# Both heads' probabilities normalised on ScalarE in the attention overlays

## The chip, the core and the metric

The kernel runs on one core of a Trainium2 chip. A core has TensorE (PE, matmuls; PEld is its weight load), VectorE (DVE), ScalarE (ACT), GpSimd (POOL) and SyncE (SP, which here only issues DMAs). Each works through its own queue in order, and they wait for each other by semaphores. The metric is the device time of one execution in microseconds, as the median over runs.

## What is computed

One layer of a decoder trunk over 2048 tokens of width 1024: a modulation by a condition vector, one wide projection, sliding-window attention with sinks beside a pooling branch, three more projections and a layer norm. The attention is the part that matters here:

```
u = x * (1 + scale) + shift
q, k, v, a_gate, p_in, p_gate, m_a, m_p = split(u @ w_in)
logits = q . k / 8 + bias            # 16 heads of 64, 2 kv heads, window 128, blocks of 128
probs  = softmax(concat(logits, sink))[..., :-1]
a      = (probs . v) * silu(a_gate)
y      = (sigmoid(m_a) * (a @ w_attn_proj) + sigmoid(m_p) * (p @ w_pool_proj)) @ w_out * (1 + gate)
out    = layer_norm(2 ** 0.25 * x + y)
```

## The kernel before

The large products are computed in fp32 by three matmuls on a high and a low part of each operand, and blocked by a Winograd scheme of seven products per two-by-two block. The activations lie in seven sets in SBUF (`set_B11` and so on), each split in a high and a low part; the weights come by DMA into `W`, POOL makes the sums and differences that the scheme needs (`W<-W`, `W<-W,A`), ACT makes the high part (`act.copy`, a cast into `w_set`) and DVE, at a few places POOL, the low part (`low`, a subtraction `w_set<-W,w_set`). As soon as the low part of the first pair is made, POOL's next difference of `W` (`mid`) may begin, since it overwrites what the split has read. The products accumulate in PSUM (`mm`, `c`, `lg`, `p` by names), and ACT and DVE take them out: `q_hi`, `q_lo`, `sig`, `px`.

A planner (`plan`) decides on which product each weight load and split is issued. `run` walks through the products; some hooks and deferred steps are issued after each.

The attention doesn't have a stage of its own. `overlay` lays it into the projection's products: `beat` is called after every three matmuls of a product, and now and then issues one `step(n)`. There are two overlays, one for each half of the tokens, with 64 steps each; a step is one pair of heads and one block of 128 queries. In the trace the first runs from about 170 to 490 us, the second from about 758 to 1075 us. `step(n)` works on four blocks at once, in this order of issue:

- PE: scores of block n into the PSUM tile `lg` (one buffer; it waits until DVE has read the scores of block n-1), the transposes of block n-2 into `pt`, and the product of block n-3 with `v` into `pv`.
- Block n-1, the lines that are changed: DVE makes the reciprocals of both heads' sums (`sm`, 128x2); ACT multiplies head 0's probabilities by the first, DVE head 1's by the second. `E` is the tile named `L` in the profile, 128 queries by 2 heads by 257 values.
- Block n-2: ACT copies the transposed probabilities to `pth` (high part).
- Block n-3: ACT copies the lower half of `pv` to `o2` (`o` in the profile).
- Block n, for both heads in turn: DVE adds the bias to the scores and takes the minimum (`tensor_tensor_reduce`; the page prints it as CUSTOM_DVE, the order as ISA), which frees `lg`; ACT takes the exponential with the sum in an accumulator.
- DVE: low part `ptl` of block n-2, and the sums `st` of block n-3.
- POOL copies the sink's value into `L` of block n+1.

Nearly every engine instruction is recorded by the helper at line 56, so all rows carry L56 and are told apart by their tiles.

## Time and profile before

| | us |
|---|---|
| median of 3 runs (1715.05 to 1715.85) | 1715.49 |
| profiled execution | 1721.38 |
| its span, first to last instruction | 1719.3 |
| clock granted to TensorE, mean | 0.989 |

A row of the groups reads: line, engine, operation, output<-inputs by the program's names, shapes, count, then busy us and mean ns of one, then the idle time of the engine ahead of them and who ended it. A row in order of time begins with the start in us and the duration; in brackets stands the idle time before it and who ended that. A row of the waits reads: who waited, for whom, us in total, times, longest. The clock is the share of full speed that TensorE was granted.

### The profile page before, as it was taken

The page shows a single profiled execution, that of the slowest core. Times are in us where ns is not written, and L with a number is a line of the kernel's source. Part 1 is how long each engine was busy: PE and PEld are TensorE (multiplying, and loading weights), DVE is VectorE, ACT ScalarE, POOL GpSimd, SP SyncE. Part 2 cuts the span into 40 slices and gives each one's busy share as a digit, 9 for nine tenths or more (in the row PEclk, how much of TensorE's full clock was granted, in tenths as well). Part 3 has the DMA queues.
Part 4 walks back from the last instruction along what each step waited for, and adds up shares of the span by engine and source line. Part 5 has one row for each costly group of instructions (what it writes and reads, how often), then busy time and mean ns, then how long its engine had stood idle before and what let it go on. Part 6 is the DMA issues. An engine that isn't in the chain of part 4 may idle for free.

```text
span 1719.3 us, 24847 instructions
## 1 busy us (share of the span) xinstructions
PE 1672.1 (97%) x8112; PEld 1400.3 (81%) x8112; DVE 1274.5 (74%) x2295; ACT 945.4 (55%) x1815; POOL 590.5 (34%) x563
## 2 busy tenths in 40 slices
PE   9899999989999999999999999999999999999997
PEld 7678788878788888888888888888878888888886
DVE  5956787778756778658877888487886785778778
ACT  3644687767753436447777676433454443434552
POOL 3012455545553223323334243322243311113544
PEclk8999999999999999999999999999999999999999
DMA  9389666766547789873555544489978695778343
GB/s 355 120 285 301 204 213 228 244 214 201 190 162 228 254 281 316 285 249 119 183 178 188 180 145 154 160 268 325 336 260 290 199 331 182 259 261 295 147 147 122
DMA packets 236545, 389.50 MB, mean 227 GB/s; under 512 B 20840, under 2 KB 90240, under 8 KB 236288
## 3 DMA queue, kind: packets, MB, share of 16 engines
q1 hardware_dynamic: 235344, 386.55, 66.9%
q10 hardware_dynamic: 1040, 1.34, 0.3%
q8 instruction: 64, 1.05, 0.3%
q14 instruction: 65, 0.53, 0.1%
q0 software_dynamic: 32, 0.02, 0.0%
HBM read 243.63 MB, written 147.35 MB: 227 GB/s over the span
## 4 chain that ended last, share of the span: by engine, by line
PE 74%; DVE 10%; DMA 6%; ACT 5%; issue 4%; SPq 1%; POOL 0%; DVEq 0%; ACTq 0%; POOLq 0%
PE mm L56 46%; PE lg L56 12%; PE c L56 10%; PE pv L56 3%; PE pt L56 3%; DVE w_set L56 3%; DVE L L56 2%; ACT L L56 2%; ACT w_set L56 1%; DVE wide L56 1%; SPq L56 1%; DMA A<-in_win_dram 1%; ACT sig L56 1%; DMA qs<-q_d 1%; ACT q_hi L56 1%
## 5 line engine op out<-in xcount | busy, mean ns | idle before, releaser
L56 PE MATMUL mm<-set_B,w_set 128*128 128x512 f32 x2664 | 655.6, 393 | 1.5 <-DVE w_set L56 1.3
L56 PEld LDWEIGHTS mm<-set_B,w_set 128*128 128x128 f32 x2664 | 498.5, 189 | 105.5 <-DVE w_set L56 2.2
L56 PE MATMUL mm<-set_T,w_set 128*128 128x512 f32 x1896 | 470.4, 395 | 1.7 <-DVE set_T L56 0.9
L56 POOL TENSOR_TENSOR W<-W 128x512 f32<-128x512 f32 x185 | 267.2, 1454 | 568.3 <-DVE w_set L56 373.7
L56 PEld LDWEIGHTS mm<-set_T,w_set 128*128 128x128 f32 x1896 | 354.9, 191 | 75.4 <-DVE set_T L56 1.6
L56 DVE TENSOR_TENSOR w_set<-W,w_set 128x1024 fp32r<-128x1024 f32 x197 | 254.7, 1293 | 111.9 <-ACT w_set L56 101.9
L56 ACT CAST w_set<-W 128x1024 fp32r<-128x1024 f32 x222 | 232.2, 1047 | 92.8 <-PE mm L56 52.9
L56 ACT ACTIVATE L<-L 128x257 f32<-128x257 f32 (+3 forms) x384 | 191.2, 500 | 117.8 <-DVE L L56 117.2
L56 PE MATMUL lg<-set_T,w_set 128*128 128x512 f32 x828 | 201.1, 390 | 4.4 <-DVE set_T L56 2.3
L56 PE MATMUL c<-set_T,w_set 128*128 128x512 f32 x828 | 199.8, 390 | 0.0
L56 PEld LDWEIGHTS lg<-set_T,w_set 128*128 128x128 f32 x828 | 155.0, 188 | 37.9 <-DVE set_T L56 3.5
L56 PEld LDWEIGHTS c<-set_T,w_set 128*128 128x128 f32 x828 | 155.0, 188 | 32.1
L56 POOL TENSOR_TENSOR W<-W,A 128x512 f32<-128x512 f32 x41 | 56.2, 1371 | 283.6 <-DMA A<-in_win_dram 135.8
L56 DVE CUSTOM_DVE_ANT_0 L<-lg,bt,nsink 128x256 f32<-128x256 f32 (+1 forms) x256 | 111.0, 470 | 23.8 <-PE lg L56 17.5
L56 DVE TENSOR_TENSOR ptl<-pt,pth 128x512 fp32r<-128x512 f32 (+1 forms) x128 | 85.8, 670 | 30.3 <-ACT pth L56 29.3
L56 PEld LDWEIGHTS lg<-kk,qs 128*128 128x128 f32 x512 | 76.5, 189 | 36.7 <-DVE L L56 26.3
L56 PE MATMUL lg<-kk,qs 128*128 128x256 f32 (+1 forms) x512 | 83.6, 286 | 18.2 <-DVE L L56 17.6
L56 DVE TENSOR_SCALAR L<-L 128x256 f32<-128x256 f32 (+1 forms) x128 | 96.9, 757 | 4.5
L56 ACT ACTIVATE sig<-mm 128x512 f32<-128x512 f32 x76 | 45.5, 599 | 96.9 <-PE mm L56 94.7
L56 ACT CAST pth<-pt 128x512 fp32r<-128x512 f32 (+1 forms) x128 | 72.4, 565 | 24.6 <-PE pv L56 23.9
L56 POOL TENSOR_TENSOR w_set<-W,w_set 128x1024 fp32r<-128x1024 f32 x25 | 61.3, 2452 | 56.8 <-ACT w_set L56 31.1
L56 PE MATMUL pv<-pth,vv 128*128 128x256 f32 x248 | 75.4, 325 | 1.9 <-DMA vv<-v_d 1.9
(208 smaller groups left out, 1957.4 us busy)
## 6 DMA issues: line engine op xcount, KB each, us to landing
W<-in_win_dram SPq DMA_DIRECT2D x40, 512.0 KB, 5.8
qs<-q_d SPq DMA_DIRECT2D x128, 128.0 KB, 4.6
sums_d<-W SPq DMA_DIRECT2D x62, 256.0 KB, 4.2
W<-sums_d SPq DMA_DIRECT2D x31, 512.0 KB, 3.6
ain_d<-st SPq DMA_DIRECT2D x56, 256.0 KB, 3.6
A<-in_win_dram SPq DMA_DIRECT2D x42, 256.0 KB, 5.8
q_d<-q_hi SPq DMA_DIRECT2D x32, 256.0 KB, 3.9
q_d<-q_lo SPq DMA_DIRECT2D x32, 256.0 KB, 4.0
```

Source lines behind the costliest of these rows:

```text
L56: return lambda *args, **kw: self.tc.keep_in_program_order(op(*args, **kw))
```

## The change

DVE's multiplication of head 1's probabilities by its reciprocal becomes a second multiplication on ACT, right behind that of head 0. The loop over the two heads takes the place of the two lines.

```
                 E, e0, sm = Es.pop(n - 1)
                 dve.reciprocal(sm, sm)
-                act.activation(E[:, 0, e0:256], E[:, 0, e0:256], AF.Copy, scale=sm[:, 0:1])
-                dve.tensor_scalar(E[:, 1, e0:256], E[:, 1, e0:256], sm[:, 1:2], None, ALU.mult)
+                for h in range(2):
+                    act.activation(E[:, h, e0:256], E[:, h, e0:256], AF.Copy, scale=sm[:, h : h + 1])
```

On DVE, in a step of the first overlay in which the weights of the projection are split just ahead of the reciprocal (the step before PE's scores at 212.84 us), the order of before is:

```order
L56 SCALAR_TENSOR_TENSOR sig<-sig,mm 128x512
L56 TENSOR_TENSOR w_set<-W,w_set 128x1024
L56 RECIPROCAL L<-L 128x2
L56 TENSOR_SCALAR L<-L 128x256
L56 ISA L<-lg,bt,nsink 128x128
L56 ISA L 128x1
L56 ISA L<-lg,bt,nsink 128x128
L56 ISA L 128x1
L56 TENSOR_TENSOR ptl<-pt,pth 128x512
```

and that of the change, at the same place:

```order
L56 SCALAR_TENSOR_TENSOR sig<-sig,mm 128x512
L56 TENSOR_TENSOR w_set<-W,w_set 128x1024
L56 RECIPROCAL L<-L 128x2
L56 ISA L<-lg,bt,nsink 128x128
L56 ISA L 128x1
L56 ISA L<-lg,bt,nsink 128x128
L56 ISA L 128x1
L56 TENSOR_TENSOR ptl<-pt,pth 128x512
```

The TENSOR_SCALAR between the reciprocal and the scores' minimum is gone.

On ACT, the same step and the one after it, as a difference (`sig` and `w_set` belong to the projection, the exponentials are the rows with 129 or 257 values):

```order
 L56 ACTIVATE sig<-mm 128x512
 L56 CAST w_set<-W 128x1024
-L56 ACTIVATE L<-L 128x256
+L56 ACTIVATE L<-L 128x256 x2
 L56 CAST pth<-pt 128x512
 L56 COPY o_1930<-pv 64x256
 L56 ACTIVATE L<-L 128x129 x2
 L56 COPY mm<-mm 128x512
-L56 ACTIVATE L<-L 128x128
+L56 ACTIVATE L<-L 128x128 x2
 L56 CAST pth<-pt 128x512
 L56 COPY o_1988<-pv 64x256
```

Each normalisation stands twice, ahead of the copies of `pt` and `pv` and the exponentials. On PE, POOL and SP the order is the same.

## The prediction

> **What bounds the kernel now.** I read the first part of the page, then the stretches of the two attention overlays, then who waits for whom, then the order of time around the waits. The page's first part (busy time, share, instructions by engine):

> ```profile
> span 1719.3 us, 24847 instructions
> PE 1672.1 (97%) x8112; PEld 1400.3 (81%) x8112; DVE 1274.5 (74%) x2295; ACT 945.4 (55%) x1815; POOL 590.5 (34%) x563
> ```

> TensorE (PE) is the bound: 47 us of the span are all that it idles, and a change on ACT and DVE can win no more than its part of these, and what the clock loses through them. The change acts only in the overlays, whose stretches read (length, then busy time of PE, PEld, DVE, ACT, POOL, the granted clock, DMA share, GB/s):

> ```profile
> 165.00:480.00 315.00, 302.37 (x1617) 257.11 (x1616) 239.71 (x631) 227.14 (x550) 153.49 (x172) 0.98 0.67 215
> 770.00:1080.00 310.00, 303.04 (x1678) 260.22 (x1679) 246.63 (x640) 227.51 (x548) 109.63 (x121) 1.00 0.50 162
> ```

> PE idles 12.6 us in the first and 7.0 us in the second. The view of waits and the groups of both overlays say at what:

> ```profile
> PE lg L56 <- DVE L L56: 17.6, 17, 3.3
> L56 PE MATMUL mm<-set_T,w_set 128*128 128x512 f32 x1323 | 329.1, 395 | 0.0
> L56 PE MATMUL mm<-set_B,w_set 128*128 128x512 f32 x1331 | 327.9, 392 | 0.0
> ```

> So 17.6 us, in 17 waits, come from one cause: the scores matmuls (`lg`) of a step wait until DVE has read the scores of the step before (one PSUM buffer). The projection's own matmuls (`mm`) wait for nothing. The longest waits and the six around 1 us, from the order of time on PE (start, duration, in brackets the idle time before):

> ```profile
> 181.28 1.12 PE L56 MATMUL lg<-kk,qs 128*128 128x256 f32 x4 [1.85 <-DVE L L56]
> 381.58 0.74 PE L56 MATMUL lg<-kk,qs 128*128 128x256 f32 x4 [3.26 <-DVE L L56]
> 412.32 0.66 PE L56 MATMUL lg<-kk,qs 128*128 128x128 f32 x4 [1.03 <-DVE L L56]
> 470.23 0.74 PE L56 MATMUL lg<-kk,qs 128*128 128x256 f32 x4 [2.14 <-DVE L L56]
> 800.80 0.74 PE L56 MATMUL lg<-kk,qs 128*128 128x256 f32 x4 [1.09 <-DVE L L56]
> 885.66 0.73 PE L56 MATMUL lg<-kk,qs 128*128 128x256 f32 x4 [1.01 <-DVE L L56]
> 890.46 0.74 PE L56 MATMUL lg<-kk,qs 128*128 128x256 f32 x4 [0.32 <-DVE L L56]
> 965.86 0.73 PE L56 MATMUL lg<-kk,qs 128*128 128x256 f32 x4 [1.16 <-DVE L L56]
> 995.42 0.74 PE L56 MATMUL lg<-kk,qs 128*128 128x256 f32 x4 [1.01 <-DVE L L56]
> 1053.05 0.74 PE L56 MATMUL lg<-kk,qs 128*128 128x256 f32 x4 [1.74 <-DVE L L56]
> ```

> Two steps in order of time, the second ending in the wait at 412.32:

> ```profile
> 404.29 0.16 DVE L56 RECIPROCAL L<-L 128x2 f32<-128x2 f32 x1
> 404.48 0.36 DVE L56 TENSOR_SCALAR L<-L 128x256 f32<-128x256 f32 x1
> 404.54 0.51 ACT L56 ACTIVATE L<-L 128x256 f32<-128x256 f32 x1 [0.18 <-DVE L L56]
> 405.08 0.59 ACT L56 CAST pth<-pt 128x512 fp32r<-128x512 f32 x1
> 405.69 0.37 ACT L56 COPY o<-pv 64x256 f32<-64x256 f32 x1
> 405.96 0.51 ACT L56 ACTIVATE L<-L 128x257 f32<-128x257 f32 x1
> 408.65 1.23 DVE L56 TENSOR_TENSOR w_set<-W,w_set 128x1024 fp32r<-128x1024 f32 x1 [0.25 <-ACT w_set L56]
> 409.79 0.16 DVE L56 RECIPROCAL L<-L 128x2 f32<-128x2 f32 x1
> 409.99 1.48 DVE L56 TENSOR_SCALAR L<-L 128x256 f32<-128x256 f32 x1
> 410.02 1.29 POOL L56 TENSOR_TENSOR W<-W 128x512 f32<-128x512 f32 x1 [1.78 <-DVE L L56]
> 410.05 0.51 ACT L56 ACTIVATE L<-L 128x256 f32<-128x256 f32 x1 [1.43 <-DVE L L56]
> 410.46 0.57 ACT L56 CAST pth<-pt 128x512 fp32r<-128x512 f32 x1
> 411.38 0.47 DVE L56 CUSTOM_DVE_ANT_0 L<-lg,bt,nsink 128x256 f32<-128x256 f32 x1
> 411.46 1.27 POOL L56 TENSOR_TENSOR W<-W,A 128x512 f32<-128x512 f32 x1
> ```

> In the first step head 1's normalisation (the TENSOR_SCALAR) takes 0.36 us. In the second it stands beside a POOL instruction that began at the same moment and ends only when that ends: 1.48 us. Both were let go by the same DVE instruction, the split of the weights at 408.65, so this is no accident. The score instruction behind it runs beside POOL at 411.46 in its usual 0.47 us. All 128 together:

> ```profile
> L56 DVE TENSOR_SCALAR L<-L 128x256 f32<-128x256 f32 (+1 forms) x128 | 96.9, 757 | 4.5
> ```

> At 0.36 each they would take 46; the other 51 us are waiting beside POOL, at 1.1 each in some 46 steps, which leaves 82 undisturbed ones.

> **The change, part by part.** It removes 128 DVE instructions and adds 128 on ACT; nothing else moves, on POOL, SP or PE.

> *Removed from DVE.* The score instruction starts where the TENSOR_SCALAR did: at 409.99 instead of 411.38, so 1.39 us earlier in a disturbed step; 0.27 (404.48 to 404.75, from the same kind of rows) in an undisturbed one.

> *Added on ACT.* One more normalisation. Its price is its spacing: 410.05 to 410.46, 0.41 us; with a short gap, 0.54 (404.54 to 405.08). I take 0.42. Behind it in ACT's queue stand the copy of the transposed probabilities, the copy of `pv`, the two exponentials, and then the projection's copies and weight casts; DVE's split of the weights waits for the casts, and the reciprocal stands behind that split. So in an undisturbed step whose chain runs over ACT the next reciprocal comes 0.42 us later. In a disturbed one ACT gives nothing away: its first exponential waited for the score instruction:

> ```profile
> L56 ACT ACTIVATE L<-L 128x257 f32<-128x257 f32 x240 | 120.6, 505 | 20.8 <-DVE L L56 20.4 <-POOL L L56 0.4
> ```

> *Sum over the 17 waits.* A wait ends earlier by 1.39, less 0.42 where the step before ran over ACT: 0.97. All 17 make 17.6; the three long ones (1.85, 3.26, 2.14) make 7.25, the fourteen short ones 10.35. Capped at 0.97, the six quoted between 1.01 and 1.74 lose 0.06, 0.12, 0.04, 0.19, 0.04 and 0.77, so 1.2: the short ones give 9.1. The long ones give 1.38 at the first (its step before had no transposes on ACT), and 0.97 twice: 3.3. Together 12.4.

> *What is late next.* PE then comes earlier to the following step, whose chain over ACT doesn't. The pair of waits at 885.66 and 890.46, 1.33 us together, shows this. Ahead of the second stands

> ```profile
> 888.32 1.28 DVE L56 TENSOR_SCALAR L<-L 128x256 f32<-128x256 f32 x1
> ```

> so its score instruction can move by 1.2 (1.28 less the 0.09 by which 1.48 and 1.39 differ), less about 0.2 that ACT adds in the disturbed step before (0.41 more, and a wait of about 0.2 to 0.5 for the score instruction gone): 1.0 of the 1.33 is kept. Nothing in the trace shows how often this bites; bounds are nothing and half (6). I take off the pair's quarter, 3.1.

> *The clock.* After the long waits the clock falls (columns as above):

> ```profile
> 180.00:195.00 15.00, 13.72 (x70) 12.06 (x71) 10.19 (x28) 10.86 (x26) 5.83 (x9) 0.89 0.30 100
> 375.00:390.00 15.00, 11.74 (x56) 9.63 (x55) 10.49 (x28) 9.81 (x23) 7.80 (x8) 0.89 0.96 337
> 465.00:480.00 15.00, 12.86 (x61) 10.60 (x60) 11.45 (x30) 10.18 (x25) 7.10 (x8) 0.89 0.43 141
> 1040.00:1060.00 20.00, 18.26 (x104) 15.57 (x103) 16.52 (x46) 14.03 (x35) 4.98 (x9) 1.00 0.33 109
> ```

> 0.11 of 15 us is 1.7 us lost after each of the waits of 1.85, 3.26 and 2.14; after 1.74 nothing. The first shrinks to about 0.5 and the third to 1.2, both under 1.74; the second stays at about 2.3. So two drops go: 3.4 us, with bounds of 0 and 5.1. [...]

> The sum: 12.4 − 3.1 + 3.4 = 12.7 us. The profiled execution took 1721.4 us, 2.1 around its span, so it would take 1708.7. The median of the runs is 1715.5, 5.9 below it; I subtract the same 12.7 there: **1703 us**, faster by 0.7%.

> **The rivals.**

> *Everything comes.* All 17.6 and three clock drops, 5.1: 22.7 us, 1693. For it speaks that PE's other waits in the overlays make only 2 us (12.6 + 7.0 − 17.6); against it that 3.26 and 2.14 are longer than the 1.39 that goes. Chance 0.10.

> *ACT takes back half.* If two undisturbed steps over ACT stand ahead of a wait, its cap is 0.55: then the seven short waits under 0.6 give their 2.5, the other seven 3.9, the long ones 1.7, together 8; less a quarter, and with one clock drop of 1.7, 7.7, and less if new waits show: 6 to 8, so 1708 to 1710. For it speaks the chain that ended last, which between 440 and 470 us runs over ACT again and again:

> ```profile
> 444.96 1.01 ACT L L56 x4
> 448.55 1.00 ACT L L56 x4
> ```

> Against it: the largest waits stand behind disturbed steps, where ACT has room. Chance 0.20.

> *The wait only changes its name.* The scores are ready sooner, and PE stands as long at the next thing, the projection's accumulators or a DMA: 1715.5. The 0.0 idle of `mm` speaks against it. The same time results if the unprofiled runs, 5.9 us shorter, don't hold these waits. Chance 0.11.

> *Slower: ACT becomes the path.* The place is PE's `mm` at the weights that ACT casts. Where an undisturbed step passes its 0.42 whole to PE, each costs 0.42; 30 such steps of the 82 eat the 12.7, and half of the 82, 17 us, gives 1720. For it: DVE's instruction takes 0.36 where undisturbed, ACT's 0.51. Against it: ACT is busy 227 of 315 us, and 128 times 0.42 in both overlays adds 27 to each, 254; and `mm` now waits 0.0. Chance 0.09. [...]

> **How the numbers follow.** The forecast has 0.50, between 1700 and 1706.5. The range is 1697 to 1713: it takes in the forecast, the half-gain, the upper part of "everything" and the edge of no change, some 0.8. A measurement of this kernel can tell about 0.2%, 3.4 us, from no change. Faster by over 0.2%: 0.50 + 0.10 + 0.20 = 0.80. Within: 0.11. Slower: 0.09.

> **What would show it.** Right: `lg` waits on DVE of 3 to 7 us instead of 17.6, the score instruction about 0.2 us behind the start of its reciprocal everywhere, two fewer stretches of clock at 0.89, and DVE's busy time down by some 97 us, ACT's up by some 64. Wrong: idle time of `mm` behind `w_set`, the reciprocal waiting longer for ACT, or score instructions that get slow beside POOL.

## The result, and the profile after

| | before | after |
|---|---|---|
| median, us (7 runs each, on one chip) | 1715.05 | 1710.46 |
| lowest to highest, us | 1713.15 to 1716.21 | 1706.22 to 1714.26 |
| ratio after/before, 95% interval | | 0.9958 (0.9942 to 0.9974) |
| profiled execution, its span, us | 1721.38, 1719.3 | 1706.22, 1704.4 |

The change makes the kernel faster by 0.4%, some 7 us by the ratio and 4.6 us by the medians. The time lies in the range; the gain is some half of the 12.7 us forecast. The page's first part after:

```profile
span 1704.4 us, 24946 instructions
PE 1662.7 (98%) x8112; PEld 1393.6 (82%) x8112; DVE 1181.2 (69%) x2167; ACT 988.1 (58%) x1943; POOL 588.2 (35%) x563
```

DVE's busy time fell by 93 us; ACT's rose by 43, less than the 64 forecast, in part since two multiplications in a row overlap (0.91 us for both in the step below, 0.51 for one in the prediction's rows). The two spans differ by 15 us, more than the runs do, because part of this lies ahead of the change. In the order of time on PE, the last wait before the first overlay, before and then after:

```profile
98.43 0.65 PE L56 MATMUL pv<-ident,vt 128*128 128x128 f32 x4 [3.77 <-ACT st L56]
```

```profile
94.04 0.66 PE L56 MATMUL pv<-ident,vt 128*128 128x128 f32 x4 [4.08 <-ACT st L56]
```

The same instructions stand 4.4 us earlier, where nothing was changed. So the kernels are compared within the overlays, and each was profiled twice (the runs e1 and e2 below). The stretches of the overlays after (columns as in the prediction):

```profile
165.00:480.00 315.00, 305.33 (x1660) 259.63 (x1659) 201.24 (x588) 253.77 (x629) 157.89 (x176) 0.99 0.67 216
770.00:1080.00 310.00, 305.30 (x1675) 262.18 (x1674) 201.41 (x559) 242.85 (x592) 114.29 (x124) 1.00 0.52 169
```

PE idles 14.4 us in the two, against 19.6 before. The view of waits says at what:

```profile
PE pt L56 <- DVE ptl L56: 8.0, 15, 0.7
...
PE lg L56 <- DVE L L56: 2.8, 4, 1.0
...
PE pt L56 <- ACT L L56: 1.3, 3, 0.7
```

The scores' wait fell from 17.6 us to 2.8, and a wait that was not there has come: the transposes (`pt`) wait until DVE has read the transposes of the step before. One such step after, in order of time:

```profile
869.45 1.23 DVE L56 TENSOR_TENSOR w_set<-W,w_set 128x1024 fp32r<-128x1024 f32 x1 [0.25 <-ACT w_set L56]
870.59 0.16 DVE L56 RECIPROCAL L<-L 128x2 f32<-128x2 f32 x1
870.67 0.47 DVE L56 CUSTOM_DVE_ANT_0 L<-lg,bt,nsink 128x256 f32<-128x256 f32 x1
870.83 1.29 POOL L56 TENSOR_TENSOR W<-W 128x512 f32<-128x512 f32 x1 [6.99 <-DVE L L56]
870.85 0.91 ACT L56 ACTIVATE L<-L 128x256 f32<-128x256 f32 x2 [1.43 <-DVE L L56]
...
871.66 0.57 ACT L56 CAST pth<-pt 128x512 fp32r<-128x512 f32 x1
871.99 0.63 PE L56 MATMUL lg<-kk,qs 128*128 128x256 f32 x4
...
872.26 0.69 DVE L56 TENSOR_TENSOR ptl<-pt,pth 128x512 fp32r<-128x512 f32 x1 [0.71 <-ACT pth L56]
...
873.01 0.66 PE L56 MATMUL pt<-ident,L 128*128 128x128 f32 x4 [0.39 <-DVE ptl L56]
```

This is the step that before ended in the wait at 885.66. The score instruction now stands directly behind the reciprocal, beside the same POOL instruction, in 0.47 us, and `lg` starts without a wait. But ACT's two multiplications, which had to wait for that reciprocal, stand ahead of its copy of `pt`; DVE's `ptl` waits 0.71 us for this copy and then reads `pt` itself until 872.95, and PE, now a microsecond earlier, has to write the next transposes there. What DVE waits for at `ptl` in both overlays, before and then after (the groups, with busy time, mean ns, idle time before them and who ended it):

```profile
L56 DVE TENSOR_TENSOR ptl<-pt,pth 128x512 fp32r<-128x512 f32 x120 | 82.4, 687 | 30.2 <-ACT pth L56 29.3
```

```profile
L56 DVE TENSOR_TENSOR ptl<-pt,pth 128x512 fp32r<-128x512 f32 x120 | 83.0, 692 | 108.3 <-ACT pth L56 108.3
```

### The profile page after: what moved, and what is told of

Read it like the earlier page. It is cut to its first block, busy times and chain, and to the rows that moved or that the text cites. A ratio compares the mean times of both kernels' runs of the same rounds, so it can differ in the third digit from the quotient of the medians.

```text
span 1704.4 us, 24946 instructions
## 1 busy us (share of the span) xinstructions
PE 1662.7 (98%) x8112; PEld 1393.6 (82%) x8112; DVE 1181.2 (69%) x2167; ACT 988.1 (58%) x1943; POOL 588.2 (35%) x563
## 4 chain that ended last, share of the span: by engine, by line
PE 71%; ACT 10%; DVE 7%; DMA 5%; issue 5%; SPq 1%; POOL 1%; DVEq 0%; ACTq 0%; POOLq 0%
PE mm L56 44%; PE lg L56 12%; PE c L56 9%; ACT L L56 5%; PE pv L56 3%; PE pt L56 3%; DVE w_set L56 2%; ACT pth L56 1%; ACT w_set L56 1%; DVE wide L56 1%; DMA head_T<-in_wada_dram 1%; SPq L56 1%; DMA W<-in_wap_dram 1%; ACT sig L56 1%; DVE ptl L56 1%
## 5 line engine op out<-in xcount | busy, mean ns | idle before, releaser
L56 PE MATMUL mm<-set_B,w_set 128*128 128x512 f32 x2664 | 653.0, 391 | 1.0 <-DVE w_set L56 1.0
L56 PEld LDWEIGHTS mm<-set_B,w_set 128*128 128x128 f32 x2664 | 496.9, 188 | 104.4 <-DVE w_set L56 2.0
L56 PE MATMUL mm<-set_T,w_set 128*128 128x512 f32 x1896 | 465.9, 392 | 3.1 <-DVE set_T L56 1.6
L56 POOL TENSOR_TENSOR W<-W 128x512 f32<-128x512 f32 x185 | 266.2, 1449 | 576.6 <-DVE w_set L56 392.3
L56 PEld LDWEIGHTS mm<-set_T,w_set 128*128 128x128 f32 x1896 | 350.7, 188 | 76.5 <-DVE set_T L56 2.6
L56 DVE TENSOR_TENSOR w_set<-W,w_set 128x1024 fp32r<-128x1024 f32 x197 | 254.4, 1291 | 110.5 <-ACT w_set L56 109.0
L56 ACT ACTIVATE L<-L 128x257 f32<-128x257 f32 (+3 forms) x512 | 241.4, 498 | 97.0 <-DVE L L56 96.4
L56 ACT CAST w_set<-W 128x1024 fp32r<-128x1024 f32 x222 | 232.3, 1047 | 93.5 <-PE mm L56 55.4
L56 PE MATMUL lg<-set_T,w_set 128*128 128x512 f32 x828 | 201.0, 390 | 4.4 <-DVE set_T L56 2.3
L56 PE MATMUL c<-set_T,w_set 128*128 128x512 f32 x828 | 199.8, 390 | 0.0
L56 PEld LDWEIGHTS lg<-set_T,w_set 128*128 128x128 f32 x828 | 154.9, 188 | 37.8 <-DVE set_T L56 3.5
L56 PEld LDWEIGHTS c<-set_T,w_set 128*128 128x128 f32 x828 | 155.0, 188 | 32.0
L56 DVE TENSOR_TENSOR ptl<-pt,pth 128x512 fp32r<-128x512 f32 (+1 forms) x128 | 86.4, 675 | 112.7 <-ACT pth L56 112.7
L56 POOL TENSOR_TENSOR W<-W,A 128x512 f32<-128x512 f32 x41 | 57.3, 1398 | 274.3 <-DMA A<-in_win_dram 90.7
L56 DVE CUSTOM_DVE_ANT_0 L<-lg,bt,nsink 128x256 f32<-128x256 f32 (+1 forms) x256 | 110.1, 467 | 25.4 <-PE lg L56 21.3
L56 ACT ACTIVATE sig<-mm 128x512 f32<-128x512 f32 x76 | 45.5, 599 | 96.4 <-PE mm L56 94.3
L56 PEld LDWEIGHTS lg<-kk,qs 128*128 128x128 f32 x512 | 77.3, 189 | 16.6 <-DVE L L56 5.9
L56 PE MATMUL pt<-ident,L 128*128 128x128 f32 x496 | 76.6, 276 | 9.4 <-DVE ptl L56 8.0
L56 PE MATMUL lg<-kk,qs 128*128 128x256 f32 (+1 forms) x512 | 81.6, 282 | 3.2 <-DVE L L56 2.8
L56 POOL TENSOR_TENSOR w_set<-W,w_set 128x1024 fp32r<-128x1024 f32 x25 | 61.0, 2440 | 63.8 <-ACT w_set L56 34.7
L56 PE MATMUL pv<-pth,vv 128*128 128x256 f32 x248 | 74.9, 323 | 1.4 <-DMA vv<-v_d 1.4
L56 DVE TENSOR_TENSOR st<-pv,o 64x128 f32<-64x128 f32 x256 | 71.2, 278 | 5.6 <-ACT o L56 3.8
```

Of the source, the lines that this page charges most:

```text
L56: return lambda *args, **kw: self.tc.keep_in_program_order(op(*args, **kw))
```

## The experiments

The theories. **A**: the overlays lost to the scores' wait, which came from POOL holding up the multiplication ahead of them; the change takes this away and gives back most of it at `pt`, which is let go late because its copy stands behind both multiplications on ACT. **B**: the waits seen were a chance of one execution. **C**: what counts is DVE's work, wherever it stands. **D, E**: ACT's length, or the place of the copy, limits by itself. **F**: the multiplication's place on DVE costs by itself, or POOL holds up any form of it. Median and ratio to before (shared runs of before on the same chip: medians 1714.84, 1714.18 and 1715.53 for e1 to e4, e5 to e8, and e9 and e10; 4 to 12 runs of each kernel), and PE's waits in the overlays, in us:

| run | edit | us | ratio (95% interval) | `lg` on DVE | `pt` on `ptl` |
|---|---|---|---|---|---|
| e1 | before again | 1714.13 | 0.9992 (0.9977 to 1.0007) | 18.0 | none |
| e2 | after again | 1708.43 | 0.9962 (0.9948 to 0.9976) | 2.9 | 8.6 |
| e3 | before, head 1 behind the scores | 1689.97 | 0.9849 (0.9829 to 0.9868) | 1.2 | 1.1 |
| e4 | after, copy of `pt` first | 1693.07 | 0.9865 (0.9845 to 0.9884) | 3.2 | none |
| e5 | after, two buffers for `pt` | 1710.42 | 0.9980 (0.9968 to 0.9992) | 2.4 | none |
| e6 | after, a third multiplication on ACT | 1759.03 | 1.0263 (1.0236 to 1.0290) | 4.8 | 39.5 |
| e7 | e3 and copy of `pt` first | 1691.54 | 0.9866 (0.9844 to 0.9887) | 0.7 | 1.1 |
| e8 | before, copy of `pt` first | 1713.08 | 0.9997 (0.9984 to 1.0010) | 13.7 | none |
| e9 | before, head 1 with one input from PSUM | 1694.80 | 0.9890 (0.9862 to 0.9918) | 3.7 | none |
| e10 | before, head 1 behind `ptl` | 1700.84 | 0.9918 (0.9899 to 0.9937) | 2.6 | 0.7 |

**Both kernels once more (e1, e2).** No edit.

> The kernel before, unchanged, for a second profile. Theory A (the overlays lost about 17 us to waits of the scores on DVE and about 5 us to clock drops; the start of the trace differs by itself between executions): PE's waits for lg on DVE again 15 to 19 us, the first scores of the first overlay anywhere between 167 and 172 us. Theory B (the 17.6 us were a chance of that one execution): these waits under 12 us. The time itself is within 0.2% of before.

> The changed kernel, unchanged, for a second profile. Theory A: waits of lg on DVE 2 to 4 us, and waits of pt on ptl 7 to 9 us again, since ACT copies pt 0.4 us later in each step and pt has one buffer; 5 to 8 us faster than before. Theory B (the 8 us of waits at pt were chance): pt waits under 4 us.

The waits come out the same, so neither was chance, and B falls. Of e1 and then of e2:

```profile
PE lg L56 <- DVE L L56: 18.0, 17, 3.4
```

```profile
PE pt L56 <- DVE ptl L56: 8.6, 16, 0.7
PE lg L56 <- DVE L L56: 2.9, 4, 1.1
```

The first scores of e1 start at 161.9 us, earlier than the 167 to 172 that I expected; before, they started at 167.9. The start does differ by itself, and by more than I had said. The view names only waits of some length. From the start times of PE's instructions, in e1 and e2: the distance from a `mm` matmul to the scores behind it makes 50.3 us in e1 and 33.1 in e2 over the 126 steps, that from the scores to the transposes behind them 15.3 and 27.7 over 122. So 17.2 us were won at `lg`, and 12.4 given back at `pt`.

**Head 1 behind the scores (e3).**

```
+            scaled = None
             if n - 1 in Es:
...
                 act.activation(E[:, 0, e0:256], E[:, 0, e0:256], AF.Copy, scale=sm[:, 0:1])
-                dve.tensor_scalar(E[:, 1, e0:256], E[:, 1, e0:256], sm[:, 1:2], None, ALU.mult)
+                scaled = E, e0, sm
...
                 Es[n] = L, e0, sm
+            if scaled:
+                E, e1, rs = scaled
+                dve.tensor_scalar(E[:, 1, e1:256], E[:, 1, e1:256], rs[:, 1:2], None, ALU.mult)
             if pt is not None:
                 low(dve, lo[:, h0:], pt[:, h0:], hi[:, h0:])
```

> The kernel before, with head 1's multiplication still on DVE, but behind the two score instructions of the step. Theory A (the scores waited for the multiplication that stood ahead of them, and what ACT got in addition costs at pt): lg waits fall to 1 to 4 us, pt waits stay under 3 us except where the multiplication is held up by POOL, 8 to 14 us faster than before and faster than the changed kernel. Rival C (what the change wins is DVE's 97 us of work, wherever they stand): within 2 us of before.

25 us faster than before, 18 faster than the changed kernel, with the split of the work of before. C falls. The multiplications are still held up:

```profile
L56 DVE TENSOR_SCALAR L<-L 128x256 f32<-128x256 f32 x120 | 79.8, 665 | 0.1
```

665 ns on average against 0.36 us undisturbed, but the scores' minimum no longer stands behind them. What does is `ptl`, and that costs PE 1.1 us at `pt`; ACT has one multiplication ahead of its copy of `pt`, as before. The gain is larger than I expected, and larger than the 18.0 us of named waits. From e1 to e3 the overlays (first to last scores of both, with what lies between) shorten by 25.1 us: 19.3 in the distance ahead of the scores, 2.3 within the scores themselves, which ran slower after a wait (0.73 us at 205.36 in e1, 0.64 without one at 165.92), 2.0 among the `mm` matmuls, where the clock fell after the long waits (three stretches of 15 us at 0.89 in e1), and the rest in small pieces. Part of it is the clock: e1 has three falls in its overlays, 5.1 us at the prediction's 1.7 each, and e3 has none.

**The copy of `pt` first (e4), and the same in the kernel before (e8).** The block that makes `hi` and `lo` and copies `pt` moves ahead of the block with the reciprocal:

```
+            if pt is not None:
...
+                act.copy(hi[:, h0:], pt[:, h0:])
             if n - 1 in Es:
                 E, e0, sm = Es.pop(n - 1)
                 dve.reciprocal(sm, sm)
...
-            if pt is not None:
...
-                act.copy(hi[:, h0:], pt[:, h0:])
```

> The changed kernel, with ACT's copy of pt into pth ahead of the two multiplications. Theory A (pt is let go late because the copy stands behind the multiplications, which wait for the reciprocal): pt waits fall from 8 us to under 2, 4 to 8 us faster than the changed kernel. Rival D (ACT's length is what counts, not the place): the time stays within 2 us of the changed kernel, and the wait moves from pt to lg or mm.

> The kernel before with nothing but the copy of pt moved ahead of head 0's multiplication. Theory A (in the kernel before the scores' wait on DVE comes last, behind the multiplication that POOL holds up; pt's release is hidden behind it): lg waits stay at 14 to 19 us, and the time within 5 us of before. Rival E (the place of the copy is what limits both kernels): 10 us or more faster than before.

On the changed kernel the move wins 15 us (1693.07 against 1708.43), more than expected, and the waits at `pt` are gone; D falls. On the kernel before it wins nothing that can be told from no change: there the scores' wait comes last, with 13.7 us left of it (14 to 19 expected), and E falls. The two conditions belong together. A step of e4 in order of time shows why the place counts, not the work:

```profile
388.65 0.59 ACT L56 CAST pth<-pt 128x512 fp32r<-128x512 f32 x1
388.74 0.15 DVE L56 RECIPROCAL L<-L 128x2 f32<-128x2 f32 x1
388.81 0.46 DVE L56 CUSTOM_DVE_ANT_0 L<-lg,bt,nsink 128x256 f32<-128x256 f32 x1
389.14 0.91 ACT L56 ACTIVATE L<-L 128x256 f32<-128x256 f32 x2
...
389.61 0.68 DVE L56 TENSOR_TENSOR ptl<-pt,pth 128x512 fp32r<-128x512 f32 x1
```

The copy runs before the reciprocal is there, in time in which ACT waited, and `ptl` follows the score instructions without a gap.

**Two buffers for `pt` (e5).** A second one in PSUM, at the price of one `pv` instead of two:

```
-            pt = ps.tile([P, 2, 2, P], F32, tag="pt", bufs=1, name="pt")
+            room, tag = (phase_ps["now"], "pt2") if n % 2 else (ps, "pt")
+            pt = room.tile([P, 2, 2, P], F32, tag=tag, bufs=1, name="pt")
...
-        phase(Pools(f"o{s}", pv=2, wx=1, p=1, c=5 if s else 4, ux=1), alone, middle(s))
+        phase(Pools(f"o{s}", pv=1, wx=1, p=1, c=5 if s else 4, ux=1), alone, middle(s))
```

> The changed kernel with a second PSUM buffer for the transposes (odd steps use one of their own), at the price of one buffer for pv instead of two. Theory A (PE stands because pt has one buffer, which ptl still reads): the waits of pt on ptl fall from 8 us to under 1, and if the single pv costs less than that, 6 to 15 us faster than the changed kernel. Rival D (the place of the copy or ACT's length delays PE by another way): the waits stay 8 us or more under another name, such as lg or mm, and the time within 3 us of the changed kernel.

The waits at `pt` vanish, so the single buffer is what PE stood at. But no time is won, where A expected 6 to 15 us: PE now waits one instruction later, at the single `pv`, which `st`, behind `ptl` on DVE, lets go. These are the numbers that the expectation gave to D, so it is e4 alone that speaks against D; and e5 can't tell whether the same lateness is met again or the lost second `pv` costs as much as the second `pt` gives.

```profile
PE pv L56 <- DVE st L56: 11.1, 19, 0.8
```

**ACT's addition doubled (e6).**

```
                 for h in range(2):
                     act.activation(E[:, h, e0:256], E[:, h, e0:256], AF.Copy, scale=sm[:, h : h + 1])
+                act.activation(E[:, 1, e0:256], E[:, 1, e0:256], AF.Copy, scale=1.0)
```

> The changed kernel with a third instruction of the same kind on ACT in each step (head 1 multiplied once more, by 1.0), so what ACT got in addition is doubled. Theory A: pth, ptl and so the release of pt come another 0.42 us later; the 16 waits at pt grow by about 0.4 each and more steps join in, to 20 us or more, and it is 8 to 20 us slower than the changed kernel, slower than before or about as before. Rival C (only DVE's side counts): within 2 us of the changed kernel.

51 us slower than the changed kernel by the medians (1759.03 against 1708.43), far beyond the 8 to 20 expected. The direction was A's, the size was not. That 128 times the 0.4 us of one multiplication is 51 as well is no explanation: from e2 to e6 the distance from the scores to the transposes grows by 38 us, practically all of it in 55 of 124 steps, by 0.2 to 1.5 us each, and in the other 69 it stays. So ACT's stretch ahead of the copy of `pt` reaches PE in less than half of the steps, and there often with more than what was added; why with more is not shown. PE's waits in the overlays of e6:

```profile
PE pt L56 <- DVE ptl L56: 39.5, 49, 1.4
PE lg L56 <- DVE L L56: 4.8, 9, 0.9
PE pt L56 <- ACT L L56: 4.7, 5, 1.4
```

**Head 1 at its old place, with one input from PSUM (e9).**

```
-                dve.tensor_scalar(E[:, 1, e0:256], E[:, 1, e0:256], sm[:, 1:2], None, ALU.mult)
+                one = E[:, 1, e0:256]
+                if lg is not None and k0_of(n) == 0:
+                    dve.scalar_tensor_tensor(one, one, sm[:, 1:2], lg[:, 1, e0:256], ALU.mult, ALU.bypass)
+                else:
+                    dve.tensor_scalar(one, one, sm[:, 1:2], None, ALU.mult)
```

> The kernel before, with head 1's multiplication at its old place on DVE but as a SCALAR_TENSOR_TENSOR whose second input is the scores in PSUM (passed by, so the same values). Theory A (the scores waited for the multiplication because POOL held it up, not for its 0.36 us): if this form isn't held up by POOL it takes 0.45 to 0.5 us in every step instead of 0.757 on average, lg waits fall from 18 us to 4 to 9, a few us of pt waits show, and it is 8 to 16 us faster than before. Rival F (the place alone costs, or POOL holds up this form as well): mean over 0.7 us, lg waits over 14 us, within 4 us of before.

As A expected, and somewhat more, without the few us of waits at `pt`: the instruction takes the same time, with no slow ones, in the 119 steps that have this form (nine keep the TENSOR_SCALAR),

```profile
L56 DVE SCALAR_TENSOR_TENSOR L<-L,lg x119: 348/482/486, 170.7 to 1041.6; 128x256 f32<-128x256 f32 x111, 128x128 f32<-128x128 f32 x8
```

(shortest, median and longest in ns), where the TENSOR_SCALAR went up to 1.48 us, beside a POOL instruction of 1.29, in the prediction's rows. In 57 of the 119 steps the new form runs beside a POOL instruction for over 0.2 us. In the trace of before the TENSOR_SCALAR took at most 0.36 us in the 55 steps with no POOL instruction beside it, and 1.19 on average in the 62 with over 0.2 us of one. With its median of 0.48 us the new form is slower than the undisturbed 0.36, stands at the same place, and the kernel is 20 us faster: the hold-up by POOL was the cost, not the place or the work. F falls. What in the form spares it, the operation or the input from PSUM, is not shown.

**Both moves, and one place later (e7, e10).** e7 puts e3 and the copy of `pt` first together; e10 puts head 1's multiplication behind `ptl` instead of ahead of it:

```
             if pt is not None:
                 low(dve, lo[:, h0:], pt[:, h0:], hi[:, h0:])
+            if scaled:
+                E, e1, rs = scaled
+                dve.tensor_scalar(E[:, 1, e1:256], E[:, 1, e1:256], rs[:, 1:2], None, ALU.mult)
```

> The split of before (head 0 on ACT, head 1 on DVE), with head 1 behind the scores on DVE and the copy of pt ahead of the normalisation on ACT. Theory A: PE's waits at lg and pt in the overlays are both under 1.5 us; 0 to 3 us faster than the kernel with head 1 behind the scores alone, since that has only about 2 us of such waits left.

> As the kernel with head 1's multiplication behind the scores on DVE, but one place later, behind the low part of the transposes (ptl), so that a hold-up by POOL no longer stands ahead of pt's release. Theory A: the 1.1 us of pt waits left there vanish, and it is 0 to 3 us faster than that kernel, 24 to 29 us faster than before, unless the transposes of the next step now wait for head 1's probabilities. Rival: no gain, 1688 to 1692 us.

e7 adds nothing to e3, as there was hardly a wait left. e10 is slower than e3, where up to 3 us faster or no gain was expected. Its proviso came true: the transposes of the next step now wait for head 1's probabilities. This is not all of the 11 us: the scores' waits are back at 2.6 us, and the clock falls twice in the first overlay (0.99 granted from 165 to 480 us, 1.00 in e3).

```profile
PE pt L56 <- DVE L L56: 4.3, 7, 0.8
```

The lowest median is e3's: 1689.97 us, 1.5% under before, and faster than the changed kernel. The intervals of e3, e4 and e7 overlap, so which of the three is fastest is open.

## Why the prediction was right, and where its size was off

*The bound and the waits* were right: 17 waits of the scores in either profile of before (17.6 and 18.0 us), and e3 and e9 show what they are worth.

*The collision with POOL* was the right cause (e9). One reading was off by an instruction: the profile has POOL let go by the reciprocal, not by the split ahead of it. POOL starts at 410.02, 0.07 us behind the reciprocal's end, and the two collide all the same.

*Removing the multiplication from DVE* gave more than the sum's 12.4 us: the named waits at `lg` fell by 14.8, to 2.8 us (3 to 7 forecast), and with what the view doesn't name the gain is 17.2. The three long waits gave 5.1 instead of 3.3; that of 3.26 us lost 2.3, more than the 1.39 that the multiplication could give, as ACT's `q_hi` ahead of it came 0.9 us earlier behind the scores of the step before. The score instruction starts 0.08 us behind the reciprocal's start, which is closer than the 0.2 forecast.

*ACT's price* was right as a duration: the copy of `pt` starts 0.81 us behind the first multiplication (870.85 to 871.66) where it was 0.41. What was wrong is where it goes. "In a disturbed one ACT gives nothing away" looked at the exponentials alone. The copy of `pt` stands ahead of them in the same queue, and behind it hang `ptl` and the release of `pt`; in the disturbed steps, where the scores came earlier, this became what PE waits for.

*What is late next* is the step of the sum that failed: 3.1 us, bounded by 6, taken from the pair at 885.66 and 890.46 and put down to later steps. Measured it is 12.4 us, at what PE does next behind the scores. 8.0 of it lie in the very steps whose scores came earlier, nearly all of the rest in seven other steps, four of them directly behind such a step. I followed `lg`'s release and ACT's chain to the next reciprocal, but not the second PSUM buffer that a step of PE needs. The rival that the wait only changes its name said this, with the projection's accumulators or a DMA as the place; `pt` was not among them, and about 70% of the gain at `lg` (12.4 of 17.2) went this way.

*The clock* was right in size, partly by luck: behind the scores' waits lie three stretches of 15 us at 0.89 in each profile of before, and one such in each of after, so two drops and 3.4 us are gone. But the drop that was to stay, behind the wait of 3.26 us, is gone, and the one behind the wait of 2.14, which was to go, is still there (at 458.15 below). One more, behind a wait of `pv` for a DMA, shows in the first profile of before and in e2 (waits of 1.95 and 2.24 us) and not in the other two (1.42 and 1.38).

With the measured terms, 17.2 − 12.4 + 3.4 gives 8.2 us; the ratio of e2 gives 6.5 of 1714.84, between 4.1 and 8.9 by its interval. That the forecast wasn't further off is luck as well: the gain at `lg` was taken 4.8 us too small, what is given back 9.3 too small. The rival that ACT takes back half gave the nearest time, 1708 to 1710; its place, chains of undisturbed steps, was for the most part not where it happened.

## What to carry to other kernels

When a wait on a bottleneck engine goes, look at every buffer that its next instructions write, and ask when each is let go; a release that comes shortly ahead of the one that was waited for doesn't show as a wait in the trace of before, and takes over at once (at `pt` none before, 8.0 us after). An instruction that waits should stand behind those in its queue that have their inputs already (15 us in e4). And before work is moved to another engine, see whether it is long because of its place or of a neighbour: here another place in the same queue was worth 25 us, moving the work 7.

## What the runs showed that I had not expected

PE's waits cost more here than their idle time: 18.0 us of named waits were worth 25, some 5 of them by the clock. The scores take 0.73 us behind a wait and 0.63 without one (885.66 in the prediction, 871.99 above).

The length of the wait alone doesn't tell in these traces whether the clock falls. In the first profile of before it did not come after 1.74 us. In e1 the same wait in the order of time and its stretch read:

```profile
1042.88 0.73 PE L56 MATMUL lg<-kk,qs 128*128 128x256 f32 x4 [1.75 <-DVE L L56]
```

```profile
1035.00:1050.00 15.00, 13.24 (x65) 11.04 (x64) 11.24 (x30) 10.95 (x27) 4.28 (x6) 0.89 0.31 105
```

And in the changed kernel two short waits in a row did it, 0.92 and 0.67 us:

```profile
458.15 0.74 PE L56 MATMUL lg<-kk,qs 128*128 128x256 f32 x4 [0.92 <-DVE L L56]
459.55 0.66 PE L56 MATMUL pt<-ident,L 128*128 128x128 f32 x4 [0.67 <-DVE ptl L56]
```

```profile
450.00:465.00 15.00, 13.40 (x61) 10.76 (x60) 9.85 (x29) 10.99 (x30) 6.91 (x8) 0.89 0.50 165
```
